# Nine adaLN steps between the output pieces of the spatial gating, attention bias rows on GpSimd's queue a head ahead, row transpositions a step later

## The chip, the cores and the metric

The kernel runs on one core of a Trainium2 chip. A core has five engines with a queue of instructions each, worked through in order: TensorE (PE; its weight loads are listed apart as PEld), VectorE (DVE), ScalarE (ACT), GpSimd (POOL) and SyncE (SP, which here only starts DMA transfers). They meet at semaphores. The metric is device time in microseconds of one execution; less is better.

## The reference: what is computed

A backbone of two layers over 512 latent tokens of width 1024, with 256 context tokens ahead of them. Layer 0 mixes by neighbourhood attention beside chunked spatial gating, layer 1 by retention; each is followed by a gated MLP with a depthwise convolution. What bears on the change:

```
mod_lat = (silu_c @ ada_w[i] + ada_b[i])         # adaLN: 6 x 1024 numbers per stream
mod_ctx = (silu_cc @ ada_w[i] + ada_b[i])        # the same for the context tokens
sh1, sc1, g1, sh2, sc2, g2 = split(mod, 6)
h = modulate(rmsnorm(x, norm_g[i, 0]), sh1, sc1)
y = hybrid_na_sgu(...) or retention_mixer(...)
x = x + g1 * rmsnorm(y, norm_g[i, 1])

# layer 0, the two branches that share one output projection
a_lat = neighbourhood_attention(q, k, v, k_ctx, v_ctx, rpb)   # bias rpb by head, row and column distance
s_lat = spatial_gating(gelu(u), gelu(g), w_s, b_s)            # u * (W_s v + b) in chunks of 128
y = concatenate([a_lat, s_lat]) @ w_out
```

The adaLN vectors depend on the conditioning alone, not on the tokens, so their work may stand anywhere ahead of its use.

## The kernel before

Tokens are held in six tiles of 128 (tiles 4 and 5 are the context). Products are made in three passes on float32r operands: each operand is split into a high part (a copy on ScalarE, line 68) and a low part (a subtraction on VectorE, line 69), and `mm3` (lines 93 to 96) multiplies high by high, high by low and low by high. Weights come in units of 128 x 1024 through three buffers of the tag `raw`, which adaLN's weight loads share.

**adaLN as background steps.** `ada_half(l, half, streams, ...)` makes 512 of the 6 x 1024 numbers of layer l. It is a generator: a call of `self.bg()` runs it to its next `yield`. One step loads a unit of weights (`ar`, issued on SP) and multiplies and adds it on VectorE into an accumulator for each stream (`acc`, line 214: with two streams four operations of 128 x 512). The accumulator is set to zero on GpSimd (line 205) and its first row is loaded with the bias (`in_adab_row`, on SP in layer 0's early halves). After four units the accumulator is split (`ah`, `al`). For the gates (halves 4, 5, 10, 11) a matmul with ones (`ag`, lines 235 and 236) sums it over the partitions and VectorE multiplies it into `G`. For the others a matmul with `sel` (`ac`, line 252) makes two rows, ScalarE copies them (`arow`, line 254), and four small transpositions (`at`, line 259) turn them into columns. When a generator ends, the same call goes on to the first step of the next. Layer 0's jobs are the halves 4, 5 (gates) and 6 to 9; in names such as `acc061`, `ar062` or `al051` the digits are layer, half, and stream or unit.

**Spatial gating (`sgu`).** After the projections and the mixing, twelve output pieces (`out_pieces`, names `wsg`: six token tiles, two halves of the width) of twelve matmuls of 128 x 512 each are run one after the other; ScalarE copies each result (`ysg`, line 492). Ahead of them the loops over the projections call `self.bg()` six times.

**Attention.** Pairs of heads are projected (`project_pair`: `pq`, `px`, `pk`, `pv`, `py`), taken out of PSUM by ScalarE and VectorE (`take_qk`: `q`, `ka`, `kb`, `vt`; GpSimd copies `kb` to its second half, line 773), and then 40 tiles (8 heads of 5 blocks) run through `score` (`s`, then the softmax in `sc` and `sst` on VectorE and ScalarE) and, two tiles later, `weigh` (transpositions `pt`, then `o` and `oc`). Projections of the next pair are filled in between. `self.bg()` is called three times in the first projection and then at every second tile. For each head `bias_tiles` loads a tile `slab` of bias rows (SP, one buffer), scales it on GpSimd (line 798) and adds the masks to make `tm` (lines 803 to 805, two buffers).

**What sets the order.** The source gives priorities, and a scheduler of the tile framework sets each engine's order by dependences, buffers and its own estimates; so a moved step can change which instruction of another kind stands ahead of it. On each engine the order is then fixed.

Retention calls `self.bg()` four times per head for the halves 4 to 9 of layer 1 with one stream; the halves 10 and 11 of both layers and 0 to 3 of layer 1 run in the ConvFFN stages.

Of the kernel before, what the change touches and what calls it, by code (L numbers as in the profile page):

```python
# [8 lines left out]
F32 = mybir.dt.float32  # L9
# [7 lines left out]
P = 128  # L17
# [13 lines left out]
RB = 32  # L31
# [9 lines left out]
class Trunk:  # L41
# [157 lines left out]
    def ada_half(self, l, half, streams, gate=None, away=False, fine=False, side=False):  # L199
        S, V, T, G = self.S, self.V, self.T, self.G  # L200
        m, h = divmod(half, 2)
        acc = []
        for s in range(streams):
            t = (self.lp if s else self.bp).tile([P, 512], F32, name=f"acc{l}{half}{s}", tag=f"acc{s}", bufs=1)
            G.memset(t, 0.0)  # L205
            (G.dma_start if side else self.load)(t[0:1], self.a["adab_row"][l * 12 + half : l * 12 + half + 1])
            acc.append(t)
        for kp in range(4):
            raw = self.bp.tile([P, 1024], F32, name=f"ar{l}{half}{kp}", tag="raw", bufs=3)
            self.load(raw, self.ada_unit_src(l, half, kp))  # L210
            for kk in range(2):
                k = kp * 2 + kk
                for s in range(streams):
                    V.scalar_tensor_tensor(  # L214
                        out=acc[s],
                        in0=raw[:, kk * 512 : kk * 512 + 512],
                        scalar=self.cs[:, 8 * s + k : 8 * s + k + 1],
                        in1=acc[s],
                        op0=ALU.mult,
                        op1=ALU.add,  # L220
                    )
                if fine and kk == 0:
                    yield
            yield
        sp = []
        for s in range(streams):
            hi = self.t2k(f"ah{l}{half}{s}", F32R)
            lo = self.t2k(f"al{l}{half}{s}", F32R)
            self.split(hi, lo, acc[s])
            sp.append((hi, lo))  # L230
            if fine:
                yield
            if m in (2, 5):
                ps = self.ps(f"ag{l}{half}{s}", "C")
                T.matmul(ps, self.ones, hi, start=True, stop=False)
                T.matmul(ps, self.ones, lo, start=False, stop=True)
                ngr = self.t2k(f"ngr{l}{half}{s}")
                row = l * 4 + (1 if m == 2 else 3)
                src = self.a["norm_g"][row : row + 1, h * 512 : h * 512 + 512].broadcast_to([P, 512])
                (G.dma_start if side else self.load)(ngr, src)  # L240
                dst = gate[s][:, h * 512 : h * 512 + 512]
                if away:
                    V.tensor_tensor(out=ngr, in0=ps, in1=ngr, op=ALU.mult)
                    G.dma_start(dst, ngr)
                else:
                    V.tensor_tensor(out=dst, in0=ps, in1=ngr, op=ALU.mult)
        if m in (2, 5):
            return
        ps = self.ps(f"ac{l}{half}", "C")
        n = 2 * streams  # L250
        for i in range(n):
            T.matmul(ps[:2], self.sel[:, i // 2, :], sp[i // 2][i % 2], start=(i == 0), stop=(i == n - 1))
        row = self.t2k(f"arow{l}{half}")
        S.copy(row[:2], ps[:2])
        if fine:
            yield
        pt = self.ps(f"at{l}{half}", "C", (P, 4, 2))
        for i in range(4):
            T.transpose(pt[:, i, :], row[:2, i * P : (i + 1) * P], self.ident[:2, :2])
        ab = self.ab[l, 0 if m < 2 else 1]  # L260
        gi = (l * 4 + (0 if m < 2 else 2)) * 8 + h * 4
        for s in range(streams):
            if m in (0, 3):
                V.tensor_copy(ab[:, s, 1, h * 4 : h * 4 + 4], pt[:, :, s])
            else:
                V.scalar_tensor_tensor(
                    out=ab[:, s, 0, h * 4 : h * 4 + 4],
                    in0=pt[:, :, s],
                    scalar=1.0,
                    in1=self.ng[:, gi : gi + 4],  # L270
                    op0=ALU.add,
                    op1=ALU.mult,
                )
# [279 lines left out]
    def sgu(self, y, xn):  # L553
        S, V, T, G, a = self.S, self.V, self.T, self.G, self.a
        toks = (4, 5, 0, 1, 2, 3)
        with ExitStack() as ctx:
# [105 lines left out]
            mix(1)  # L662
            turn(1)
            pieces = self.out_pieces([(st[0][:, f, :], st[1][:, f, :]) for f in range(4)], wo, y, toks, True, None, "sg")
            for f in pieces:
                f()

    def attention(self, y, final):
        a = self.a
        with ExitStack() as ctx:  # L670
            ap = self.ap = self.phase(ctx, "attp", 0)
            self.mask = ap.tile([P, 3, 256], F32, name="mask", tag="mask")
            self.load(self.mask, a["mask"])
            self.pt_all = ap.tile([P, 4, 4, P], F32, name="ptall", tag="ptall")
            pairs = [{} for _ in range(4)]
            heads = [{} for _ in range(8)]
# [10 lines left out]
            for i in range(n + lag):  # L687
                if i < n:
                    h, b = tiles[i]
# [91 lines left out]
    def take_v(self, j, pr):  # L781
        vn = pr["vn"] = self.ap.tile([P, 6, P], F32, name=f"vn{j}", tag="vn", bufs=1)
        for i, n in ((0, 4), (4, 2)):
# [4 lines left out]
                )  # L788
            self.S.copy(vn[:, i : i + n, :], pv[:, : n * P].rearrange("p (b c) -> p b c", b=n))

    def bias_tiles(self, h, hd):

        G, ap = self.G, self.ap
        tm = hd["tm"] = ap.tile([P, 3, 256], F32, name=f"tm{h}", tag="tm", bufs=2)
        slab = ap.tile([P, 256], F32, name=f"slab{h}", tag="slab", bufs=1)
        z = self.a["rpb"]
        self.load(slab, bass.AP(z.tensor, RB + h * 15 * RB - 8, [[RB, 8], [1, 16], [1, 256]]))
        G.tensor_scalar(out=slab, in0=slab, scalar1=8.0, scalar2=0.0, op0=ALU.mult, op1=ALU.add)
        sr = slab.rearrange("p (r i) -> p i r", r=8)[:, ::-1, ::-1]
        t3 = tm.rearrange("p v (i r) -> p v i r", r=8)  # L800
        m3 = self.mask.rearrange("p v (i r) -> p v i r", r=8)
        for v in range(2):
            G.tensor_tensor(out=t3[:, v], in0=sr, in1=m3[:, v], op=ALU.add)
        G.tensor_tensor(out=t3[:, 2, 0:16], in0=sr[:, 16:32], in1=m3[:, 2, 0:16], op=ALU.add)
        G.tensor_tensor(out=t3[:, 2, 16:32], in0=sr[:, 0:16], in1=m3[:, 2, 16:32], op=ALU.add)

    def score(self, h, b, pr, hd):

# [924 lines left out]
```

## Time and profile before

| what | us |
|---|---|
| median of 3 runs | 1904.04 (1901.92 to 1905.67) |
| the profiled execution | 1893.99 |
| its span on the core | 1892.2 |
| first and last matmul start of the output pieces `wsg` | 118.4, 153.9 |
| first and last matmul start of the scores `s` | 192.8, 365.9 |
| first and last addition of retention's output `yr` (before its last group) | 1119.5, 1395.4 |

The mean granted clock of TensorE in that execution was 0.983 of full speed. In the rows of the profile a name such as `acc<-ar,cs,acc` is output and inputs, `128x512` partitions by elements, and what stands in brackets at a row's end is how long the engine had been idle before it and what ended the wait. A row of the timeline begins with the start and the duration in us. Waits are put down to the semaphore event that came last, so a wait that names an engine which had long been done was for something else, often a DMA.

### The profile page before, as it was taken

The page shows a single profiled execution, that of the slowest core. Times are in us where ns is not written, and L with a number is a line of the kernel's source. Part 1 is how long each engine was busy: PE and PEld are TensorE (multiplying, and loading weights), DVE is VectorE, ACT ScalarE, POOL GpSimd, SP SyncE. Part 2 cuts the span into 40 slices and gives each one's busy share as a digit, 9 for nine tenths or more (in the row PEclk, how much of TensorE's full clock was granted, in tenths as well). Part 3 has the DMA queues.
Part 4 walks back from the last instruction along what each step waited for, and adds up shares of the span by engine and source line. Part 5 has one row for each costly group of instructions (what it writes and reads, how often), then busy time and mean ns, then how long its engine had stood idle before and what let it go on. Part 6 is the DMA issues. An engine that isn't in the chain of part 4 may idle for free. (4 is left out here: it accounts for less than half of the span.)

```text
span 1892.2 us, 28751 instructions
## 1 busy us (share of the span) xinstructions
PE 1800.1 (95%) x10928; PEld 1591.7 (84%) x10928; DVE 1402.8 (74%) x2352; ACT 1029.2 (54%) x1857; POOL 325.8 (17%) x446
## 2 busy tenths in 40 slices
PE   7998989979999999999989999999999989999998
PEld 4886867669889899998879889988989779889996
DVE  4844788679877778777877666675665689989877
ACT  6533545666555555555565434434444377666763
POOL 1102122130122222222121010011011100222221
PEclk9999999999999999999989999999999989999999
DMA  7333332132577877776744313322421225878772
GB/s 290 115 100 106 93 101 79 57 136 76 175 176 156 184 158 167 145 169 135 232 146 131 119 52 112 112 95 62 134 66 48 100 81 148 212 188 195 178 162 99
DMA packets 83823, 250.32 MB, mean 132 GB/s; under 512 B 10578, under 2 KB 12114, under 8 KB 83684
## 3 DMA queue, kind: packets, MB, share of 16 engines
q1 hardware_dynamic: 58436, 200.72, 32.8%
q0 software_dynamic: 25248, 47.75, 15.2%
q8 instruction: 86, 1.41, 0.3%
q14 instruction: 53, 0.43, 0.1%
HBM read 191.81 MB, written 39.85 MB: 122 GB/s over the span
## 5 line engine op out<-in xcount | busy, mean ns | idle before, releaser
L214 DVE SCALAR_TENSOR_TENSOR acc<-ar,cs,acc 128x512 f32<-128x512 f32 x256 | 189.5, 758 | 35.5 <-DMA ar<-in_adaw 19.7
L1463 POOL DMA_DIRECT2D yf<-yp x64 | 55.9, 873 | 260.2 <-ACT yp L1459 229.2
L1314 ACT ACTIVATE cv<-pre,cw 128x770 f32<-128x770 f32 (+1 forms) x88 | 80.9, 923 | 27.2 <-DVE pre L1307 25.9
L1315 DVE SCALAR_TENSOR_TENSOR cv<-pre,cw,cv 128x769 f32<-128x769 f32 (+1 forms) x88 | 77.2, 880 | 7.2 <-ACT cv L1314 7.2
L1459 ACT COPY yp<-wf 128x512 f32<-128x512 f32 x118 | 67.9, 577 | 18.1 <-PE wf L96 18.0
L1318 DVE SCALAR_TENSOR_TENSOR cv<-pre,cw,cv 128x769 f32<-128x769 f32 (+1 forms) x88 | 77.2, 881 | 0.7
L1302 ACT ACTIVATE pre<-px 128x256 f32<-128x256 f32 (+2 forms) x160 | 54.3, 367 | 41.8 <-PE px L93 33.6
L1098 POOL TENSOR_SCALAR rrr<-rmv 128x2 f32<-128x2 f32 x16 | 3.1, 193 | 363.2 <-DVE rmv L1095 363.2
L1463 POOL DMA_DIRECT2D yd<-ypg x48 | 42.1, 903 | 132.1 <-ACT ypg L1459 130.6
L1463 POOL DMA_DIRECT2D yd<-yp x48 | 42.6, 902 | 126.7 <-ACT yp L1459 126.6
L68 ACT ACTIVATE g<-cv 128x770 fp32r<-128x770 f32 (+1 forms) x44 | 32.5, 738 | 32.6 <-DVE cv L1322 32.4
L93 PE MATMUL px<-hs,wd 128*128 128x384 f32 x240 | 45.4, 337 | 0.0
L93 PEld LDWEIGHTS px<-hs,wd 128*128 128x128 f32 x240 | 42.3, 188 | 1.9 <-DVE pre L1307 0.4
L1307 DVE TENSOR_TENSOR pre<-pre,pz 128x256 f32<-128x256 f32 (+1 forms) x60 | 20.8, 371 | 29.2 <-PE pz L96 29.1
L69 DVE TENSOR_TENSOR g<-cv,g 128x770 fp32r<-128x770 f32 (+1 forms) x44 | 36.1, 821 | 7.4 <-ACT g L68 7.3
L1302 ACT ACTIVATE pre<-py 128x384 f32<-128x384 f32 (+1 forms) x40 | 17.5, 437 | 43.9 <-DVE cv L1318 25.6
L1322 DVE TENSOR_TENSOR cv<-cv 128x770 f32<-128x770 f32 (+1 forms) x44 | 36.2, 822 | 4.3 <-ACT cv L1321 3.1
L1321 ACT ACTIVATE cv<-cv 128x770 f32<-128x770 f32 (+1 forms) x44 | 32.7, 742 | 11.7 <-DVE cv L1318 11.6
L1078 DVE SCALAR_TENSOR_TENSOR of<-rx,e,of 128x256 f32<-128x256 f32 x64 | 28.9, 477 | 8.4 <-PE rx L96 7.9
L869 ACT ACTIVATE sc<-sc,sst 128x512 f32<-128x512 f32 x32 | 23.0, 719 | 22.1 <-DVE sc L860 21.6
L1459 ACT COPY ypg<-wf 128x512 f32<-128x512 f32 x54 | 30.7, 578 | 6.5 <-PE wf L96 6.4
L205 POOL MEMSET acc<- 128x512 f32 x32 | 19.1, 600 | 84.5 <-DVE al L69 62.2
(2985 smaller groups left out, 7181.1 us busy)
## 6 DMA issues: line engine op xcount, KB each, us to landing
ar<-in_adaw SPq DMA_DIRECT2D x96, 512.0 KB
yf<-yp POOLq DMA_DIRECT2D x64, 256.0 KB, 4.2
yd<-yp POOLq DMA_DIRECT2D x54, 256.0 KB, 5.2
yd<-ypg POOLq DMA_DIRECT2D x54, 256.0 KB, 5.0
fin<-xd SPq DMA_DIRECT2D x10, 512.0 KB
xd<-xd SPq DMA_DIRECT2D x8, 512.0 KB
xn<-in_x SPq DMA_DIRECT2D x6, 512.0 KB
xb<-in_x SPq DMA_DIRECT2D x6, 512.0 KB
```

Of the source, the lines that this page charges most:

```text
L68: self.S.activation(hi, src, AF.Copy)
L69: self.V.tensor_tensor(out=lo, in0=src, in1=hi.bitcast(F32), op=ALU.subtract)
L93: mm = lambda *p, **k: self.nc.tensor.matmul(*p, skip_group_check=True, **k)
L214: V.scalar_tensor_tensor(out=acc[s], in0=raw[:, kk * 512 : kk * 512 + 512], scalar=self.cs[:, 8 * s + k : 8 * s + k + 1], in1=acc[s], op0= ...
L1302: S.activation(pre[:, i, c : c + w], ps[:, b : b + w], AF.Copy, scale=scale)
L1314: S.activation(d, s, AF.Identity, scale=w1, bias=b)
L1315: V.scalar_tensor_tensor(out=d[:, 1:W], in0=s[:, 0 : W - 1], scalar=w0, in1=d[:, 1:W], op0=ALU.mult, op1=ALU.add)
L1318: V.scalar_tensor_tensor(out=d[:, 0 : W - 1], in0=s[:, 1:W], scalar=w2, in1=d[:, 0 : W - 1], op0=ALU.mult, op1=ALU.add)
L1321: S.activation(cv[:, 0], cv[:, 0], AF.Silu)
L1322: V.tensor_tensor(out=cv[:, 0], in0=cv[:, 0], in1=cv[:, 1], op=ALU.mult)
L1459: S.copy(v, ps)
L1463: G.dma_start((yd[t] if first else y[t])[:, o], v, accum_op=ALU.add)
```

## The change

Three edits. `ada_half` yields between the copy of the row and its transpositions in every job, not only in those called `fine`; a half that isn't a gate so takes five steps instead of four. In `sgu` the loop over the twelve output pieces calls `self.bg()` after each of the first nine. In attention the load of a bias slab moves from SP to GpSimd's queue (`load_slab`), and is issued for the next head at the end of `bias_tiles`, the first one ahead of the loop.

```diff
--- before.py
+++ after.py
@@ -252,8 +252,7 @@
             T.matmul(ps[:2], self.sel[:, i // 2, :], sp[i // 2][i % 2], start=(i == 0), stop=(i == n - 1))
         row = self.t2k(f"arow{l}{half}")
         S.copy(row[:2], ps[:2])
-        if fine:
-            yield
+        yield
         pt = self.ps(f"at{l}{half}", "C", (P, 4, 2))
         for i in range(4):
             T.transpose(pt[:, i, :], row[:2, i * P : (i + 1) * P], self.ident[:2, :2])
@@ -662,8 +661,10 @@
             mix(1)
             turn(1)
             pieces = self.out_pieces([(st[0][:, f, :], st[1][:, f, :]) for f in range(4)], wo, y, toks, True, None, "sg")
-            for f in pieces:
+            for i, f in enumerate(pieces):
                 f()
+                if i < 9:
+                    self.bg()
 
     def attention(self, y, final):
         a = self.a
@@ -671,6 +672,7 @@
             ap = self.ap = self.phase(ctx, "attp", 0)
             self.mask = ap.tile([P, 3, 256], F32, name="mask", tag="mask")
             self.load(self.mask, a["mask"])
+            self.load_slab(0)
             self.pt_all = ap.tile([P, 4, 4, P], F32, name="ptall", tag="ptall")
             pairs = [{} for _ in range(4)]
             heads = [{} for _ in range(8)]
@@ -788,13 +790,16 @@
                 )
             self.S.copy(vn[:, i : i + n, :], pv[:, : n * P].rearrange("p (b c) -> p b c", b=n))
 
+    def load_slab(self, h):
+        self.slab = self.ap.tile([P, 256], F32, name=f"slab{h}", tag="slab", bufs=1)
+        z = self.a["rpb"]
+        self.G.dma_start(self.slab, bass.AP(z.tensor, RB + h * 15 * RB - 8, [[RB, 8], [1, 16], [1, 256]]))
+
     def bias_tiles(self, h, hd):
 
         G, ap = self.G, self.ap
         tm = hd["tm"] = ap.tile([P, 3, 256], F32, name=f"tm{h}", tag="tm", bufs=2)
-        slab = ap.tile([P, 256], F32, name=f"slab{h}", tag="slab", bufs=1)
-        z = self.a["rpb"]
-        self.load(slab, bass.AP(z.tensor, RB + h * 15 * RB - 8, [[RB, 8], [1, 16], [1, 256]]))
+        slab = self.slab
         G.tensor_scalar(out=slab, in0=slab, scalar1=8.0, scalar2=0.0, op0=ALU.mult, op1=ALU.add)
         sr = slab.rearrange("p (r i) -> p i r", r=8)[:, ::-1, ::-1]
         t3 = tm.rearrange("p v (i r) -> p v i r", r=8)
@@ -803,6 +808,8 @@
             G.tensor_tensor(out=t3[:, v], in0=sr, in1=m3[:, v], op=ALU.add)
         G.tensor_tensor(out=t3[:, 2, 0:16], in0=sr[:, 16:32], in1=m3[:, 2, 0:16], op=ALU.add)
         G.tensor_tensor(out=t3[:, 2, 16:32], in0=sr[:, 0:16], in1=m3[:, 2, 16:32], op=ALU.add)
+        if h < 7:
+            self.load_slab(h + 1)
 
     def score(self, h, b, pr, hd):
 
```

By the count of steps, layer 0's jobs ended before in the sixteenth of the calls in attention's loop, and now in the eleventh, with 15 calls instead of 6 ahead of attention. In retention the last step moves from the first call of head 6 to the first call of head 7. Line numbers of the changed kernel are up to seven higher in what follows (`score` L813 is L820, `weigh` L883 is L890), but the transpositions of the row, L259, are L258.

*First place: TensorE, the fourth output piece `wsg51` (token tile 5, second half).* Before:

```order
L94 MATMUL wsg51_1385<-wos2h_1287,sT0_703 128x512
L95 MATMUL wsg51_1385<-wos2l_1288,sT0_703 128x512
L96 MATMUL wsg51_1385<-wos2h_1287,sT1_704 128x512
L94 MATMUL wsg51_1385<-wos3h_1293,sT0_703 128x512
L95 MATMUL wsg51_1385<-wos3l_1294,sT0_703 128x512
L96 MATMUL wsg51_1385<-wos3h_1293,sT1_704 128x512
L94 MATMUL wsg00_1400<-wos0h_1275,sT0_703 128x512
L95 MATMUL wsg00_1400<-wos0l_1276,sT0_703 128x512
```

In the changed kernel:

```order
L94 MATMUL wsg51_1429<-wos2h_1287,sT0_703 128x512
L95 MATMUL wsg51_1429<-wos2l_1288,sT0_703 128x512
L235 MATMUL ag050_1401<-ah050_1397,ones_88 128x512
L96 MATMUL wsg51_1429<-wos2h_1287,sT1_704 128x512
L235 MATMUL ag051_1411<-ah051_1407,ones_88 128x512
L236 MATMUL ag050_1401<-al050_1398,ones_88 128x512
L94 MATMUL wsg51_1429<-wos3h_1293,sT0_703 128x512
L95 MATMUL wsg51_1429<-wos3l_1294,sT0_703 128x512
L236 MATMUL ag051_1411<-al051_1408,ones_88 128x512
L96 MATMUL wsg51_1429<-wos3h_1293,sT1_704 128x512
L94 MATMUL wsg00_1450<-wos0h_1275,sT0_703 128x512
```

The four gate matmuls of half 5 now stand in the end of this piece, ahead of eight more pieces; those of half 6 (`ac06`) come in the piece `wsg21` and its transpositions in `wsg30`.

*Second place: TensorE at the end of the first pair's projection, `pv0` and `py0`.* Before:

```order
L96 MATMUL pv0_1652<-h0a_116,wv0l_1538 128x512
L235 MATMUL ag050_1681<-ah050_1677,ones_88 128x512
L236 MATMUL ag050_1681<-al050_1678,ones_88 128x512
L235 MATMUL ag051_1691<-ah051_1687,ones_88 128x512
L94 MATMUL py0_1709<-h0a_116,wv0h_1537 128x256
L95 MATMUL py0_1709<-h1a_117,wv0h_1537 128x256
```

and, nine rows further on:

```order
L95 MATMUL py0_1709<-h1a_117,wv0h_1537 128x256
L96 MATMUL py0_1709<-h0a_116,wv0l_1538 128x256
L94 MATMUL py0_1709<-h0a_116,wv0h_1537 128x256
L236 MATMUL ag051_1691<-al051_1688,ones_88 128x512
L95 MATMUL py0_1709<-h1a_117,wv0h_1537 128x256
L96 MATMUL py0_1709<-h0a_116,wv0l_1538 128x256
L94 MATMUL py0_1709<-h0a_116,wv0h_1537 128x256
```

In the changed kernel:

```order
L96 MATMUL pv0_1756<-h0a_116,wv0l_1642 128x512
L252 MATMUL ac07_1789<-ah070_1781,sel_90 2x512
L252 MATMUL ac07_1789<-al070_1782,sel_90 2x512
L252 MATMUL ac07_1789<-ah071_1785,sel_90 2x512
L252 MATMUL ac07_1789<-al071_1786,sel_90 2x512
L94 MATMUL py0_1796<-h0a_116,wv0h_1641 128x256
L95 MATMUL py0_1796<-h1a_117,wv0h_1641 128x256
```

Half 5's gate matmuls are gone from here (the last of them stood inside `py0`); the row matmuls of half 7 stand ahead of `py0`. SyncE's queue for the same time, before, from the first weight unit of half 6:

```order
L54 DMA ar060_1703<-in_adaw 128x1024
L54 DMA slab0_1793<-in_rpb 128x1x256
L54 DMA wq1r_1772<-in_hyb_qkv 128x1024
L54 DMA slab1_2028<-in_rpb 128x1x256
L54 DMA wk1r_1778<-in_hyb_qkv 128x1024
L54 DMA ngr050_1684<-in_norm_g 128x512
L54 DMA acc060_1697<-in_adab_row 1x512
L54 DMA slab2_2272<-in_rpb 128x1x256
L54 DMA wv1r_1784<-in_hyb_qkv 128x1024
L54 DMA ar061_1874<-in_adaw 128x1024
L54 DMA ngr051_1694<-in_norm_g 128x512
L54 DMA acc061_1700<-in_adab_row 1x512
```

In the changed kernel, from the third unit of half 7:

```order
L54 DMA ar072_1670<-in_adaw 128x1024
L54 DMA ar073_1726<-in_adaw 128x1024
L54 DMA wq1r_1859<-in_hyb_qkv 128x1024
L54 DMA wk1r_1865<-in_hyb_qkv 128x1024
L54 DMA wv1r_1871<-in_hyb_qkv 128x1024
L54 DMA acc080_1968<-in_adab_row 1x512
L54 DMA ar080_1974<-in_adaw 128x1024
L54 DMA acc081_1971<-in_adab_row 1x512
L54 DMA ar081_2076<-in_adaw 128x1024
L54 DMA ar082_2187<-in_adaw 128x1024
L54 DMA ar083_2273<-in_adaw 128x1024
```

The bias slabs have left this queue, and the weights of pair 1 follow the adaLN loads directly.

*Third place: VectorE at the softmax of head 1's fourth block (`sc13`).* Before, from behind its first instruction to its last:

```order
L771 TENSOR_TENSOR kb11_2148<-pk1_1892,ka11_2147 64x448
L264 COPY ab01_97<-at06_2188 128x4 x2
L214 SCALAR_TENSOR_TENSOR acc070_2195<-ar070_2201,cs_75,acc070_2195 128x512
L771 TENSOR_TENSOR kb11_2148<-px1_1849,ka11_2147 64x256
L771 TENSOR_TENSOR kb11_2148<-pk1_1892,ka11_2147 64x64
L214 SCALAR_TENSOR_TENSOR acc071_2198<-ar070_2201,cs_75,acc071_2198 128x512
L214 SCALAR_TENSOR_TENSOR acc070_2195<-ar070_2201,cs_75,acc070_2195 128x512
L214 SCALAR_TENSOR_TENSOR acc071_2198<-ar070_2201,cs_75,acc071_2198 128x512
L870 RECIPROCAL sst13_2209<-sst13_2209 128x1
L823 TENSOR_REDUCE sst14_2227<-s14_2225 128x2
L871 TENSOR_SCALAR sc13_2208<-sc13_2208,sst13_2209 128x512
```

In the changed kernel:

```order
L69 TENSOR_TENSOR at10_1878<-oc0_2212,at00_1877 64x256
L830 TENSOR_REDUCE sst14_2299<-s14_2297 128x2
L763 TENSOR_TENSOR q11_2246<-pq1_1899,q11_2246 64x512
L766 TENSOR_TENSOR q11_2246<-px1_1936,q11_2246 64x256
L773 TENSOR_TENSOR kb11_2248<-pk1_1992,ka11_2247 64x448
L773 TENSOR_TENSOR kb11_2248<-px1_1936,ka11_2247 64x256
L877 RECIPROCAL sst13_2281<-sst13_2281 128x1
L831 TENSOR_SCALAR sst14_2299<-sst14_2299 128x2
L69 TENSOR_TENSOR al081_2340<-acc081_1971,ah081_2339 128x512
L878 TENSOR_SCALAR sc13_2280<-sc13_2280,sst13_2281 128x512
L773 TENSOR_TENSOR kb11_2248<-pk1_1992,ka11_2247 64x64
```

Before, four accumulations of half 7 stood between the two parts of this softmax; now none stands there, and half 9's follow behind head 2's first block. On GpSimd's queue the load of `slab4` and its scaling now stand between the two memsets of half 9's accumulators, and the scaling of `slab2` ahead of those of half 8.

## The prediction

> **What bounds the kernel now.** I read the page first (busy shares), then the waits of TensorE (PE) in the stretch that the change touches, then busy time in slices there, then the timeline of single engines around each wait.
>
> ```profile
> span 1892.2 us, 28751 instructions
> PE 1800.1 (95%) x10928; PEld 1591.7 (84%) x10928; DVE 1402.8 (74%) x2352; ACT 1029.2 (54%) x1857; POOL 325.8 (17%) x446
> ```
> PE is busy 95% of the span: the kernel is a queue of matmuls, and an edit is worth the PE time that it frees. The change neither adds nor removes a matmul, so only PE's waits count. PE's waits between 100 and 420 us (engine, line, waited for: us in total, times, longest):
>
> ```profile
> PE ag L236 <- DVE al L69: 8.9, 1, 8.9
> PE ht L407 <- DVE ysg L336: 6.5, 3, 4.2
> PE py L94 <- ACT vt L778: 4.4, 2, 3.8
> PE pt L883 <- DVE sst L824: 2.0, 1, 2.0
> ```
> `ht` lies behind attention, in code that the change leaves alone. The other three lie where adaLN steps and bias rows are moved. Slices of 10 us (PE busy, PEld, DVE, ACT, POOL, then the granted clock, DMA share, GB/s):
>
> ```profile
> 140.00:150.00 10.00, 10.00 (x45) 8.07 (x44) 0.00 (x0) 2.00 (x4) 0.00 (x0) 1.00 0.00 0
> 180.00:190.00 10.00, 1.10 (x10) 0.89 (x8) 4.63 (x10) 3.24 (x10) 2.00 (x3) 0.70 0.47 145
> 240.00:250.00 10.00, 7.72 (x41) 4.92 (x40) 9.90 (x28) 3.61 (x10) 2.15 (x1) 1.00 0.36 107
> 270.00:280.00 10.00, 6.21 (x36) 5.45 (x35) 5.31 (x13) 5.77 (x13) 2.26 (x2) 0.83 0.32 93
> ```
> At 140 us, among the output pieces, PE is full and VectorE (DVE) and the DMA engines do nothing: room for adaLN. In attention DVE runs at up to 9.90 of 10 and PE waits.
>
> **Wait 1, 181 to 190 us.**
>
> ```profile
> 190.05 0.80 PE L236 MATMUL ag<-al,ones 128*128 128x512 f32 x1 [8.95 <-DVE al L69]
> 191.29 0.41 PE L95 MATMUL py<-h1a,wv0h 128*128 128x256 f32 x1
> 191.50 0.41 PE L96 MATMUL py<-h0a,wv0l 128*128 128x256 f32 x1
> ...
> 200.55 0.28 PE L95 MATMUL px<-h1a,wq1h 128*128 128x256 f32 x1
> 200.66 0.28 PE L96 MATMUL px<-h0a,wq1l 128*128 128x256 f32 x1
> ```
> PE stands 8.95 us inside `py0` for half 5's last gate matmul. Afterwards matmuls start every 0.21 us instead of 0.11; by the clock (0.50 up to 194) that lasts some 4 us, half of it lost. Price of wait 1: 8.95 + 2.0 = **11.0 us**. Its chain on SyncE's queue (SP), POOL and DVE:
>
> ```profile
> 179.05 0.54 POOL L805 TENSOR_TENSOR tm<-slab,mask 128x128 f32<-128x128 f32 x1
> 179.61 0.64 SPq L54 DMA_DIRECT2D slab<-in_rpb  x1
> 180.87 0.36 SPq L54 DMA_DIRECT2D ar<-in_adaw  x1
> 187.93 0.75 DVE L214 SCALAR_TENSOR_TENSOR acc<-ar,cs,acc 128x512 f32<-128x512 f32 x1 [3.80 <-DMA ar<-in_adaw]
> 189.31 0.68 DVE L69 TENSOR_TENSOR al<-acc,ah 128x512 fp32r<-128x512 f32 x1
> ```
> A bias-row load (`slab2`) sits on SP until GpSimd (POOL) has finished the bias tiles of head 1; the adaLN load behind it goes out at 180.87 and lands 7.1 us later; DVE, in order, waits for it ahead of the split `al051` that PE wants. The change takes out both links: half 5 is finished among the output pieces, and bias rows leave SP. Four matmuls of half 7 (`ac07`) take this place in PE's order, but behind them DVE has eight accumulations whose loads wait for no bias row.
>
> **Wait 2, 243 us.**
>
> ```profile
> 238.12 0.75 DVE L214 SCALAR_TENSOR_TENSOR acc<-ar,cs,acc 128x512 f32<-128x512 f32 x1 [2.74 <-DMA acc<-in_adab_row]
> 242.17 0.48 DVE L871 TENSOR_SCALAR sc<-sc,sst 128x512 f32<-128x512 f32 x1
> 242.79 0.63 PE L883 MATMUL pt<-ident,sc 128*128 128x128 f32 x4 [1.99 <-DVE sst L824]
> ```
> PE waits 1.99 us for the softmax of head 1's fourth block (`sc13`); DVE had lost 2.74 us to half 7's bias row and about 2.8 to four accumulations just ahead of it. In the new order none stands between `sc13`'s first and last instruction (third place above). Price **2.0 us**; the clock stayed at 1.00.
>
> **Wait 3, 271 to 275 us.**
>
> ```profile
> 264.82 0.63 SPq L54 DMA_DIRECT2D slab<-in_rpb  x1
> 265.54 0.41 SPq L54 DMA_DIRECT2D wk3r<-in_hyb_qkv  x1
> 271.04 1.06 ACT L68 ACTIVATE wk3h<-wk3r 128x1024 fp32r<-128x1024 f32 x1 [2.85 <-DMA wk3r<-in_hyb_qkv]
> 274.88 0.39 PE L94 MATMUL py<-h0a,wv2h 128*128 128x256 f32 x1 [3.79 <-ACT vt L778]
> ```
> The same knot: weight `wk3` queued behind `slab5`, ScalarE (ACT) waits for it with the copies of pair 2 behind it, PE waits for those. 3.79 us, and the 0.83 of that slice's clock is 1.7 us more, 1.5 of them after the wait: **5.3 us**. With `slab` gone from SP, `wk3r` follows `wq3r` directly. The same wait one pair later, where no load was late, is the row below, so 0.6 stays and 4.7 goes.
>
> ```profile
> 325.31 0.39 PE L94 MATMUL py<-h0a,wv3h 128*128 128x256 f32 x1 [0.57 <-ACT vt L778]
> ```
> Sum of what goes: 11.0 + 2.0 + 4.7 = 17.7 us.
>
> **What the change adds, part by part.**
>
> *Nine steps between pieces.* They bring eight units of adaLN weights (512 KB each), 32 accumulations, the splits of halves 5 and 6, eight matmuls on a [128x512] row and four small transposes. These only change place; counted with attention, PE's work is the same. What they can add is a wait where PE now reaches an adaLN matmul before DVE.
>
> ```profile
> 161.88 5.53 DVE L214 SCALAR_TENSOR_TENSOR acc<-ar,cs,acc 128x512 f32<-128x512 f32 x8 [2.18 <-DMA ar<-in_adaw]
> ...
> 126.52 0.41 DVE L69 TENSOR_TENSOR sT<-st3C,sT 128x256 fp32r<-128x256 f32 x1
> 156.09 1.23 DVE L69 TENSOR_TENSOR wq0l<-wq0r,wq0h 128x1024 fp32r<-128x1024 f32 x1 [29.16 <-ACT wq0h L68]
> ...
> 150.82 0.59 ACT L492 COPY ysg<-wsg 128x512 f32<-128x512 f32 x1 [2.21 <-PE wsg L96]
> 153.61 0.59 ACT L492 COPY ysg<-wsg 128x512 f32<-128x512 f32 x1 [2.21 <-PE wsg L96]
> ```
> One step is four accumulations of 5.53/8 = 0.69 us, 2.8 us; one piece is 153.61 - 150.82 = 2.79 us. DVE is free from 126.9 to 156.1, 29 us. The two match, so each handover is close:
> - Gate matmuls in `wsg51`: from 126.9, eight accumulations end at 132.5, splits (0.64 on ACT, 0.68 each on DVE) at 134.5. PE would get there at 133 to 134. I take 1.0 us. Below: 0. Above: if both loads take the 7.1 us of the row at 180.87 instead of the 3.6 of the rows below, 4.5.
>
> ```profile
> 115.62 0.33 SPq L54 DMA_DIRECT2D wos1r<-in_hyb_out  x1
> 119.20 1.06 ACT L68 ACTIVATE wos1h<-wos1r 128x1024 fp32r<-128x1024 f32 x1 [2.13 <-DMA wos1r<-in_hyb_out]
> ```
> - Row matmuls `ac06` in `wsg21`: the new accumulator's memset and bias row cost some 2.7 us (the wait of 2.74 above), 16 accumulations 11.1, splits 2: ready at 150.3. PE, with 1.9 us of gate matmuls and wait ahead of it, starts `wsg21` at 150. I take 0.5; 0 to 4.
> - Attention's first weight `wq0l` on DVE, now behind six accumulations of half 7: ready at 160.2 by the same sum, and PE, delayed by twelve moved matmuls and these waits, wants it at 161. I take 0.5; 0 to 4.
>
> *Bias rows on POOL's queue, a head ahead.* SP is rid of eight issues that blocked it. On POOL the issue is hidden under its own idle time (17% busy), but POOL is in order, so what stands behind `slab` waits for its landing: the memsets of `acc08` now stand behind the scaling of `slab2`, then comes their bias row on SP, and `ar080` behind that. In my sum `acc08` starts at 186.5, 4.6 us after DVE ran dry; its 16 accumulations are woven into the first two score tiles, and PE, at `s03`, waits for `sc01` to give its bank back: about 2.5 us. Bounds 0 to 5.4, the latter with the cold clock of wait 3.
>
> The rows show that POOL and DVE slow each other: the same tile operation on POOL takes 870 to 1393 ns.
>
> ```profile
> L803 POOL TENSOR_TENSOR tm<-slab,mask x16: 870/1039/1393, 167.0 to 336.2; 128x256 f32<-128x256 f32 x16
> ```
> The Trainium skill, "SBUF — State Buffer", section "SBUF: two separate sides", says that DVE and GpSimd share one pair of ports under an exclusive lock, and that a DMA issued from GpSimd can starve while DVE holds it. By that rule `slab2`'s issue meets the accumulations of half 7 and lands later; if by two of them (2 x 0.69), `acc08` and `s03` slip by 1.4 us and the sum below is 11.8 instead of 13.2. The row above agrees that the two block each other; no row here shows a slab issue on POOL.
>
> ```profile
> 185.56 0.41 POOL L798 TENSOR_SCALAR slab<-slab 128x256 f32<-128x256 f32 x1 [5.98 <-DMA slab<-in_rpb]
> ```
> POOL waited 6.0 us for this slab. Twice that fits in a head, which lasts (336.2 - 167.0)/7 = 24 us by the tile row's first and last start, so the bias tiles themselves stay early and I add nothing for them.
>
> *Transposes a step later.*
>
> ```profile
> PEld at L259 <- ACT arow L254: 1.3, 4, 0.4
> ```
> The weight loads of the transposes stood 1.3 us in all for the row copy, mostly under a running matmul. I count nothing; bounds -1 to +1. In retention the same edit pushes up to four steps back, into stages like this one, where PE has nothing to gain and DVE has 24 us free of 50; zero, -1 to +2.
>
> ```profile
> 1400.00:1450.00 50.00, 50.00 (x372) 47.23 (x371) 26.20 (x48) 21.69 (x30) 4.51 (x7) 1.00 0.21 65
> ```
> **Sum.** 17.7 - (1.0 + 0.5 + 0.5 + 2.5) = 13.2, so 13 us. The profiled execution (1893.99 us) would become 1881. It is 10 us below the median of the runs shown (1904.04), and the same 13 us off the median give **1891**. ConvFFN stages keep their order.
>
> **Rivals.**
> 1. *The waits move instead of going* (0.20). Wait 1 is taken, but the bias row of `acc09` (its second half stands behind `slab4`) and the late `acc08` make PE stand at `s03` and once more, each past 3.8 us with a cold stretch (2 x 5.3), which more than gives back waits 2 and 3: 17.7 - 2.0 - 10.6 = 5, 1899. For it: DVE's 9.90. Against: some 30 accumulations leave attention. By the Trainium skill, "TensorE: Matmul & The Clock Gate", section "What's actually happening", idling through a window of about 3.4 us halves the clock; waits 2 (1.99, clock 1.00) and 3 (3.79, 0.83) agree, and a new wait of 2 us costs only itself.
> 2. *The stall at `py0` doesn't go* (0.07): `ac07` waits there as `ag05` did, because its loads come late through three shared buffers. Then only waits 2 and 3 are gained, 6.7 - 4.5 = 2: 1902.
> 3. *Slower* (0.06): the DVE chain from 126.9 to `wq0l`. Where PE waits over 3.8 us at each of the three handovers, each costs up to 4.2 + 1.6 cold, 17 in all; with the `s03` wait and waits 2 and 3 unchanged, 11.0 - 17.4 - 2.5 = 9 lost: 1913. It decides once loads land in 7 us instead of 3.6 and DVE gets less than one step per piece. Against: 0.00 DMA share among the pieces.
> 4. *More* (0.07): no new wait at all, the 0.6 us left of wait 3 goes too, and the transposes bring 1 us: 17.7 + 1.6 = 19.3, 1884.7.
>
> **How the numbers follow.** Forecast 0.60: 1887 to 1896, 1891 likeliest. With rival 1 and 4, and most of 2, the range is 1884 to 1902; outside lie rival 3, the top of 2 and some of 4, under 0.2. About 0.2%, 3.8 us, is what a measurement of this kernel can tell from none: faster means below 1900.2. That is forecast and rival 4, 0.67, and three quarters of rival 1, 0.15: 0.82. Same: 0.12 (rival 2 and the rest of 1). Slower: 0.06.
>
> **What would show it.** PE busy above 9.5 of 10 through 180 to 190 with the clock at 1.00, no `slab` on SP, DVE full between 127 and 160, `ac07` without a wait, PE's wait for `vt` under 1 us. Waits of PE for `al` in `wsg51` or `wsg21` above 2 us, for `wq0l`, or at `s03` above 3 us, would make the sum too large; a cold clock at any of them would make it wrong.

## The result and the profile after

| | before | after | ratio |
|---|---|---|---|
| median, runs on one chip | 1903.27 (5 runs, 1899.35 to 1905.67) | 1886.78 (5 runs, 1882.18 to 1895.16) | 0.9927, 95% 0.9902 to 0.9953 |
| the same once more (run 6 below) | 1902.92 (11 runs) | 1884.46 (6 runs, 1880.91 to 1891.07) | 0.9904, 95% 0.9881 to 0.9928 |
| profiled execution | 1893.99 | 1886.89 | |

The changed kernel is 14 to 18 us faster, by the two ratios. Its page, first lines (span, then the busy time of each engine, its share, and the instructions):

```profile
span 1884.7 us, 28785 instructions
...
PE 1801.3 (96%) x10928; PEld 1594.7 (85%) x10928; DVE 1404.0 (74%) x2352; ACT 1028.8 (55%) x1857; POOL 325.9 (17%) x454
```
The busy times are those of before; what shrank is waiting. PE's waits between 100 and 420 us, the two longest (engine, line, waited for: us in total, times, longest):

```profile
PE ht L406 <- DVE ysg L335: 6.0, 3, 3.9
PE pq L94 <- ACT ka L774: 4.7, 1, 4.7
```
The waits for `al` (8.9), `vt` (4.4) and `sst` (2.0) are gone, and a new one of 4.7 us stands at `pq`, the first product of pair 1. The same slices of 10 us as before (busy us of PE, PEld, DVE, ACT and POOL, then PE's granted clock, DMA share, GB/s):

```profile
140.00:150.00 10.00, 10.00 (x45) 7.95 (x44) 9.91 (x16) 2.78 (x5) 0.00 (x0) 1.00 0.45 130
180.00:190.00 10.00, 6.82 (x42) 5.38 (x41) 5.02 (x9) 4.51 (x11) 3.45 (x6) 1.00 0.36 118
190.00:200.00 10.00, 8.07 (x32) 6.64 (x33) 9.91 (x20) 5.61 (x11) 3.93 (x1) 0.83 0.46 129
200.00:210.00 10.00, 10.00 (x63) 8.73 (x63) 7.77 (x22) 2.94 (x6) 0.00 (x0) 1.00 0.60 186
...
240.00:250.00 10.00, 9.93 (x60) 6.91 (x58) 9.94 (x22) 3.43 (x8) 0.00 (x0) 1.00 0.35 105
270.00:280.00 10.00, 9.89 (x58) 6.72 (x57) 7.74 (x23) 6.80 (x14) 2.04 (x2) 1.00 0.14 52
```
DVE, idle at 140 before, is full there now, and PE stays full beside it. At 240 and 270 PE went from 7.72 and 6.21 to 9.9. What is left is the hole from 187 to 192. Its chain, from the timelines of POOL, SP, DVE, ACT and PE:

```profile
180.91 0.63 POOL L796 DMA_DIRECT2D slab<-in_rpb  x1 [0.30 <-POOL tm L810]
184.24 0.40 POOL L803 TENSOR_SCALAR slab<-slab 128x256 f32<-128x256 f32 x1 [2.69 <-DMA slab<-in_rpb]
184.69 0.99 POOL L205 MEMSET acc<- 128x512 f32 x2
...
185.24 0.24 SPq L54 DMA_DIRECT2D acc<-in_adab_row  x1
185.59 0.33 SPq L54 DMA_DIRECT2D ar<-in_adaw  x1
...
189.34 1.42 DVE L214 SCALAR_TENSOR_TENSOR acc<-ar,cs,acc 128x512 f32<-128x512 f32 x2 [4.02 <-DMA ar<-in_adaw]
190.79 0.43 DVE L766 TENSOR_TENSOR q<-px,q 64x256 fp32r<-64x256 f32 x1
...
191.25 0.38 ACT L772 ACTIVATE ka<-px 64x256 fp32r<-64x256 f32 x1 [4.89 <-DVE q L766]
191.65 0.22 ACT L774 ACTIVATE ka<-pk 64x64 fp32r<-64x64 f32 x1
...
191.93 0.80 PE L94 MATMUL pq<-h0a,wq1h 128*128 128x512 f32 x1 [4.68 <-ACT ka L774]
```
Read it downwards. POOL, in order, waits for `slab2` before it zeroes half 8's accumulators. SP, in order, sends their bias row only then, and `ar080` behind it. DVE, in order, stands 4.02 us for `ar080`, with the split `q10<-px0` behind. ACT waits for that split with the last reader of `pk0` behind it, and PE needs this bank for `pq1`. Four queues, each in order, make a load of adaLN, whose matmuls `ac08` PE runs only at 235.66, hold up attention.

To compare kernels free of what happens later, I take the start of the first ConvFFN matmul, `pf`, whose group's row gives the first and last start (before, then after):

```profile
L94 PE MATMUL pf<-hb,wp00h x16: 276/338/522, 411.0 to 1522.0; 128*128 128x384 f32 x8, 128*128 128x256 f32 x8
```
```profile
L94 PE MATMUL pf<-hb,wp00h x16: 274/334/542, 396.4 to 1512.8; 128*128 128x384 f32 x8, 128*128 128x256 f32 x8
```
Up to there the change saves 411.0 - 396.4 = 14.6 us. From there to the end of the span it seems to lose seven (1892.2 - 411.0 = 1481.2, against 1488.3); run 6 settles that.

### The profile page after: what moved, and what is told of

It is laid out like the page before. It is cut to its first block, busy times and chain, and to the rows that moved or that the text cites. A ratio compares the mean times of both kernels' runs of the same rounds, so it can differ in the third digit from the quotient of the medians.

```text
span 1884.7 us, 28785 instructions
## 1 busy us (share of the span) xinstructions
PE 1801.3 (96%) x10928; PEld 1594.7 (85%) x10928; DVE 1404.0 (74%) x2352; ACT 1028.8 (55%) x1857; POOL 325.9 (17%) x454
## 5 line engine op out<-in xcount | busy, mean ns | idle before, releaser
L1466 ACT COPY yp<-wf 128x512 f32<-128x512 f32 x118 | 67.8, 577 | 17.7 <-PE wf L96 17.6
L205 POOL MEMSET acc<- 128x512 f32 x32 | 19.3, 606 | 150.3 <-DVE al L69 131.6
L69 DVE TENSOR_TENSOR rv<-rn,rv 128x512 fp32r<-128x512 f32 x24 | 16.5, 687 | 29.5 <-ACT rv L68 29.5
L68 ACT ACTIVATE rv<-rn 128x512 fp32r<-128x512 f32 x24 | 14.3, 595 | 41.9 <-PE rn L96 41.9
```

What stands on the lines that cost most here:

```text
L68: self.S.activation(hi, src, AF.Copy)
L69: self.V.tensor_tensor(out=lo, in0=src, in1=hi.bitcast(F32), op=ALU.subtract)
L1466: S.copy(v, ps)
```

## The experiments

All runs, in one table (steps: calls among the pieces; later: transpositions a step later; rows: the queue of the bias rows; zero: the engine that zeroes half 8's accumulators). Runs 1 to 4, 5 to 8 and 9 to 12 were each taken together on one chip, with runs of the kernel before beside them.

| run | steps | later | rows | zero | median us | ratio to before, 95% | `pf` at |
|---|---|---|---|---|---|---|---|
| before | 0 | no | SP | POOL | 1902 to 1903 | 1 | 411.0 |
| 9 | 0 | yes | SP | POOL | 1903.15 | 1.0005, 0.9985 to 1.0025 | 411.0 |
| 12 | 9 | no | SP | POOL | 1895.98 | 0.9975, 0.9955 to 0.9994 | 403.5 |
| 1 | 0 | yes | POOL | POOL | 1908.49 | 1.0024, 1.0005 to 1.0043 | 416.9 |
| 3 | 9 | no | POOL | POOL | 1896.13 | 0.9969, 0.9948 to 0.9991 | 405.7 |
| 2 | 9 | yes | SP | POOL | 1886.01 | 0.9912, 0.9885 to 0.9940 | 396.4 |
| change, 6 | 9 | yes | POOL | POOL | 1886.78, 1884.46 | 0.9927, 0.9904 | 396.4, 399.4 |
| 4 | 7 | yes | POOL | POOL | 1890.75 | 0.9931, 0.9906 to 0.9956 | 399.8 |
| 7 | 7 | no | POOL | POOL | 1891.40 | 0.9934, 0.9912 to 0.9957 | 400.2 |
| 8 | 9 | yes | SP | DVE | 1885.69 | 0.9908, 0.9888 to 0.9928 | 397.9 |
| **5** | 9 | yes | POOL | DVE | **1879.97** | 0.9876, 0.9853 to 0.9899 | 391.2 |
| 11 | as 5, `kb` copies on ACT | | | | 1882.67 | 0.9906, 0.9880 to 0.9932 | 394.3 |
| 10 | 0 | yes | POOL | DVE (halves 6 to 8) | 1899.37 | 0.9991, 0.9972 to 1.0010 | 408.4 |

Median less the start of `pf` (one profile each) is 1485 to 1493 in every row, while `pf` itself moves by 26 us, so most of what tells these kernels apart happens ahead of `pf`.

**Run 1: without the steps.**

```diff
-            for i, f in enumerate(pieces):
+            for f in pieces:
                 f()
-                if i < 9:
-                    self.bg()
```


> The change without the nine adaLN steps; bias rows on GpSimd's queue and the later transpositions stay. The prediction's working says that wait 1 hung on two links, a bias row ahead of the adaLN load on SyncE's queue and half 5's gate matmuls standing inside py0. With one link gone the load goes out some 5 us earlier, so that wait 1 shrinks from 8.95 us to 3 to 5 us and its cold stretch goes; wait 3 (3.79 us at py2) goes to under 1 us; wait 2 (2 us) stays. Gain on the kernel before 8 to 12 us, about 1893. Rival (the queue is not what matters, only the room among the pieces): wait 1 stays above 7 us, the gain is 4 to 5 us, 1898.

Slower than the kernel before; both theories fell. Timelines of POOL, SP, DVE and PE:

```profile
182.46 0.40 POOL L801 TENSOR_SCALAR slab<-slab 128x256 f32<-128x256 f32 x1 [2.87 <-DMA slab<-in_rpb]
182.92 0.53 POOL L205 MEMSET acc<- 128x512 f32 x1
...
183.47 0.24 SPq L54 DMA_DIRECT2D acc<-in_adab_row  x1
...
184.82 0.75 DVE L214 SCALAR_TENSOR_TENSOR acc<-ar,cs,acc 128x512 f32<-128x512 f32 x1 [8.08 <-DMA acc<-in_adab_row]
...
194.98 0.79 PE L236 MATMUL ag<-al,ones 128*128 128x512 f32 x1 [13.72 <-DVE al L69]
```
This is the chain of `pq1` again with half 6 in the place of half 8: zeroing behind `slab2`, the row behind the zeroing, DVE's queue behind the row, and `al051` in that queue. Taking the slab off SP didn't break the link; it moved to POOL's queue, where it holds longer (8.95 us of wait before, 13.72 here). Wait 3 went as the theory said, and wait 2, which was to stay, went too.

**Run 2: bias rows as before** (`load_slab` undone; steps and later transpositions stay).

> The change with the bias rows as before, on SyncE's queue and in their own head; the nine steps and the later transpositions stay. Theory (rows on SyncE hold up weights behind them): the new wait at pq1 shrinks, since acc08's memsets stand ahead of slab2 here, but a weight of pair 2 or 3 is held behind slab3 to slab5, and PE waits some 4 us there, as at py2 before: about 3 us slower than the changed kernel, 1890. Rival (the steps alone reorder the queue enough): wk3 now stands ahead of slab5, no weight is late, and the knot at pq1 is gone as well: 4 to 6 us faster than the changed kernel, 1882.

As fast as the changed kernel, where the theory had it 3 us slower, so the rows' move to POOL is worth nothing that these runs can tell. PE waited 1.6 us at `pq` and 2.9 at `s` instead of 4.7 at `pq`: the same knot, against the rival, which was right on the weights. SP's timeline:

```profile
234.22 0.62 SPq L54 DMA_DIRECT2D slab<-in_rpb  x1
...
246.11 0.35 SPq L54 DMA_DIRECT2D wq3r<-in_hyb_qkv  x1
249.99 0.33 SPq L54 DMA_DIRECT2D wk3r<-in_hyb_qkv  x1
...
260.53 0.64 SPq L54 DMA_DIRECT2D slab<-in_rpb  x1
```
With the adaLN jobs further on, `wk3r` stands ahead of `slab5` (before: behind it, at 265.54), and wait 3 is gone with the slabs still on SP.

**Run 3: transpositions in the same step** (`if fine:` back ahead of the `yield`).

> The change with the row transpositions in the same step as before in attention and retention; steps and bias rows as changed. The prediction counted this part at nothing (-1 to +1): then this run is equal to the changed kernel, 1886 to 1888, with a wait of some 4.7 us at pq1. Rival: one step fewer before attention brings all eight accumulations of acc08's first two loads ahead of the split kb00<-pk0 on VectorE, so that the late load holds the whole split of keys: PE waits 8 to 11 us at pq1 with a cold stretch behind it, 6 to 8 us slower than the changed kernel, 1894.

The time is the rival's, spread over more places than it said. PE's waits between 155 and 215 us, and ACT's timeline:

```profile
PE s L821 <- ACT ka L775: 3.6, 1, 3.6
PE pq L94 <- ACT wq0h L68: 3.2, 1, 3.2
PE pq L94 <- ACT vt L781: 2.4, 1, 2.4
```
```profile
192.77 1.06 ACT L68 ACTIVATE wk1h<-wk1r 128x1024 fp32r<-128x1024 f32 x1 [10.72 <-DMA wk1r<-in_hyb_qkv]
```
One step less per row job brings all later adaLN work forward: a unit of half 7 now stands ahead of `wq0r` on SP, and half 8's bias rows ahead of `wk1r`, which goes out at 189.09 instead of 173.05; PE waits for these weights.

**Run 4: seven steps** (`if i < 7:`).

> The change with seven steps among the pieces instead of nine (one number). On VectorE acc08's accumulations now stand behind the last split for pair 0 (kb10<-px0), and its memsets behind the casts on GpSimd. Theory (the wait of 4.7 us at pq1 is the load of acc08 in VectorE's order): PE's wait at pq1 goes to under 0.5 us, the clock stays at 1.00 through 190 to 200, and the kernel is 4 to 6 us faster than the changed one, 1881 to 1883. Rival (pq1 waits for a bank that the splits give back late in any case): the wait stays above 3 us and the time is within 2 us of the changed kernel's.

The wait at `pq1` is gone as the theory said, the time isn't: between two score tiles DVE stands for `ar082` and then runs its four accumulations, 3.1 us, and PE meets that at the transposition of the values (timelines of DVE and PE):

```profile
207.13 1.42 DVE L214 SCALAR_TENSOR_TENSOR acc<-ar,cs,acc 128x512 f32<-128x512 f32 x2 [2.29 <-DMA ar<-in_adaw]
...
212.28 0.69 PE L788 MATMUL vn<-ident,vt 128*128 128x128 f32 x2 [5.29 <-ACT ptall L891]
```
Moving the late accumulations moves the wait.

**Run 5: half 8 zeroed on VectorE.**

```diff
-            G.memset(t, 0.0)
+            (V if (l, half) == (0, 8) else G).memset(t, 0.0)
```


> The changed kernel, with half 8's two accumulators zeroed on VectorE instead of GpSimd; nothing else. In the changed kernel's trace they are zeroed on GpSimd at 184.69, behind the scaling of slab2 that had waited 2.69 us for its load, and the bias row and ar080 go out on SyncE behind that. Here they are zeroed at about 182, and ar080 stands ahead of the bias row on SyncE. Theory (GpSimd's order behind slab2 sets acc08, acc08 holds the splits of pair 0 on VectorE, these hold pq1's bank): VectorE's wait of 4.0 us for ar goes to under 1 us, PE's wait at pq1 from 4.7 to under 1 us, the clock stays at 1.00, 5 to 6 us faster than the changed kernel, 1881. Rival (the time comes back: PE reaches the scores 6 us sooner and VectorE, in its order, does not): a wait of 3 to 5 us at a score or value tile between 200 and 215 us as with seven steps, 1885 to 1887.

As the theory said. DVE's timeline and two slices:

```profile
182.45 0.48 DVE L205 MEMSET acc<- 128x512 f32 x1 [0.17 <-DVE q L763]
...
186.34 0.74 DVE L214 SCALAR_TENSOR_TENSOR acc<-ar,cs,acc 128x512 f32<-128x512 f32 x1
187.11 0.43 DVE L766 TENSOR_TENSOR q<-px,q 64x256 fp32r<-64x256 f32 x1
```
```profile
180.00:190.00 10.00, 8.74 (x52) 7.15 (x51) 9.56 (x18) 6.95 (x18) 5.18 (x6) 1.00 0.45 120
190.00:200.00 10.00, 10.00 (x62) 8.78 (x61) 9.97 (x21) 3.18 (x5) 3.46 (x1) 1.00 0.66 189
```
The accumulation starts at 186.34 without a wait, the split follows at 187.11 instead of 190.79, PE has no wait left at `pq`, and only 1.3 us at `s` for `kb`. This kernel beats the changed one by 4.5 us of median on the same chip (1877.76 to 1881.16 against 1880.91 to 1891.07); the intervals of the two ratios overlap a little, but `pf` starts at 391.2, 5 us and more ahead of both profiles of the change.

**Run 6: the change again.**

> The changed kernel itself once more, to have it on the same chip as the others. Theory: 0.991 to 0.994 of the kernel before, with the first matmul of ConvFFN's block 0 (pf) at 396 to 397 us of the span, as in the first profile, and the stretch from there to the end anywhere between 1481 and 1495 us, which is what the six profiles so far show of work in one and the same order. Rival (the change slows ConvFFN): that stretch is over 1488 us again.

The rival fell: from `pf` to the end it takes 1880.7 - 399.4 = 1481.3 us here, as before the change; over the ten profiles with the later transpositions, and so with one order from `pf` on (the change, runs 1, 2, 4 to 6 and 8 to 11), it is anywhere from 1481 to 1495; over the four with the order of before (before, runs 3, 7 and 12) from 1481 to 1493. So the seven microseconds need no cause in the change, and the kernel before had a lucky execution (1893.99 against a median of 1903). The theory missed the start of `pf`, by 3 us, and the ratio, 0.9904, by a little: the wait at `pq` was 4.8, nearly the same, with one of 1.3 for `kb` just ahead of it, but the clock behind it stayed low far longer (slices of its profile):

```profile
180.00:190.00 10.00, 7.65 (x46) 6.08 (x44) 6.10 (x9) 4.52 (x11) 5.19 (x7) 0.98 0.25 71
190.00:200.00 10.00, 6.18 (x15) 4.94 (x16) 8.67 (x17) 4.92 (x10) 3.93 (x1) 0.51 0.43 147
```

**Run 7: seven steps, transpositions in the same step** (`if i < 7:`, and `if fine:` as in run 3), so that half 8 stands on DVE as in the changed kernel.

> Seven steps among the pieces and row transpositions in the same step as before; bias rows as changed. On VectorE acc08 then stands where it does in the changed kernel (two accumulations ahead of q10<-px0), against eight ahead of kb00<-pk0 with nine steps and early transpositions. Theory (the later transpositions count only as two steps of the sequence): equal to the changed kernel or up to 3 us faster, since ar080 stands ahead of the bias row here; 1884 to 1887, no wait of PE above 5 us between 155 and 210. Rival (the transposition itself, waiting for its row copy in PE's order, is what costs): as with nine steps and early transpositions, 1894 to 1897, with a wait at the transposition of 1 us and more.

Between the two. Timelines of ACT and PE:

```profile
203.09 1.04 ACT L68 ACTIVATE wq2h<-wq2r 128x1024 fp32r<-128x1024 f32 x1
204.04 0.56 ACT L254 COPY arow<-ac 2x512 f32<-2x512 f32 x1
...
204.65 0.40 PE L259 MATMUL at<-ident,arow 2*128 2x2 f32 x4 [3.51 <-ACT arow L254]
```
So the later transpositions do two things. They count as steps (run 3 against run 7: 5 us of median, though not taken side by side), and they keep PE from standing at `at` while ACT has the row copy behind other work, 3.51 us here and a cold stretch (TensorE at half clock) behind it. PE also waits 3.5 us at `s` for `kb` here, and no run shows how much of the 7 us to the changed kernel each makes.

**Run 8: rows on SyncE, zeroed on VectorE** (run 2 with the line of run 5).

> Bias rows on SyncE in their own head, as before the change, and half 8's accumulators zeroed on VectorE; steps and transpositions as changed. Theory (two links in a row, the zeroing on GpSimd and the queue on SyncE): with the zeroing gone from GpSimd the row slab2 on SyncE still waits for the bias tiles of head 1 (until about 183), ar080 behind it lands at about 187.5, and PE still waits 3 to 4 us at pq1 or for the keys: 1885, within 2 us of the same kernel with zeroing on GpSimd. So the bias rows' move is worth some 5 us, but only together with the zeroing on VectorE. Rival (the zeroing alone is the knot): as good as the changed kernel with zeroing on VectorE, 1881.

As the theory said; PE waits 1.0 us at `pq` and 3.9 at `s`. SP and DVE:

```profile
183.88 0.63 SPq L54 DMA_DIRECT2D slab<-in_rpb  x1
184.61 0.40 SPq L54 DMA_DIRECT2D ar<-in_adaw  x1
...
190.33 0.82 DVE L214 SCALAR_TENSOR_TENSOR acc<-ar,cs,acc 128x512 f32<-128x512 f32 x1 [4.40 <-DMA ar<-in_adaw]
```
Two links in a row: against run 2, which has both, taking out either one alone (the change: SP; run 8: the zeroing) gains nothing; taking out both (run 5) gains 5 us.

**Run 9: the later transpositions alone, on the kernel before.**

> The kernel before, with the later transpositions alone. Theory (they matter only where the steps have pulled a transposition among work that it can hold up): within 3 us of the kernel before, 1900 to 1905, with the wait of 8.9 us at half 5's gate matmul unchanged. Rival (each transposition that waits for its row copy costs PE, in retention too): 4 us faster or more, 1898 or less.

No difference, as expected, but not because nothing happened. Slices of its profile:

```profile
240.00:250.00 10.00, 10.00 (x60) 7.35 (x58) 9.92 (x28) 3.27 (x7) 0.00 (x0) 1.00 0.29 84
270.00:280.00 10.00, 9.88 (x59) 6.94 (x58) 7.13 (x23) 6.73 (x15) 1.37 (x2) 1.00 0.19 53
...
340.00:350.00 10.00, 6.76 (x42) 4.86 (x40) 9.64 (x28) 6.37 (x14) 0.00 (x0) 0.92 0.34 93
```
Waits 2 and 3 are gone here too, but as much is lost later, in waits for the softmax among others: from 325 to 365 us PE loses 8.0 us to idling and the half clock, against 2.0 before (8.53 of 10 in the slice from 340 before, 6.76 here). Runs 1 and 10, which also lack the steps, show the same 8 us there; in the changed kernel it is 0.9.

**Run 10: no steps, halves 6 to 8 zeroed on VectorE.**

> The change without the nine steps (that was 1908), with the accumulators of halves 6, 7 and 8 zeroed on VectorE. Theory (the wait of 13.7 us at half 5's gate matmul came from acc06, zeroed on GpSimd behind slab2 at 182.92, which held VectorE's queue for 8.1 us ahead of al051): the 8.1 us wait of VectorE goes to under 1 us, al051 ends at 187 to 188 instead of 194.9, PE waits 6 to 7 us there; 6 to 9 us faster than without the zeroing, 1900 to 1903, still 13 us and more behind the kernel that has the steps too. Rival (al051 is late because of VectorE's own load in attention): wait at the gate matmul over 11 us, 1906 and more.

Theory right, and the wait shrank further than it said: `al` is split at 186.72, PE's wait at `ag` is 4.8 instead of 13.7. Zeroing on GpSimd behind a slab cost 6 us there by the two ratios, 9 by the medians, which were taken on two chips; the steps stay worth about 20 (0.9991 against 0.9876; here halves 6 and 7 are zeroed on VectorE as well).

**Run 11: `kb` copies on ScalarE,** on top of run 5 (`S.copy` for `G.tensor_copy` at the end of `take_qk`).

> The changed kernel with half 8 zeroed on VectorE (that was 1880), and the copies of the keys' low halves (kb) on ScalarE instead of GpSimd. In the traces such a copy takes GpSimd 0.82 us, but 3.9 to 4.6 us where VectorE's accumulations run beside it, and PE waited 1.3 us for it at the first score tile. Theory (the two engines slow each other): that wait goes, VectorE's accumulations there lose nothing, 1 to 2 us faster, 1878 to 1880. Rival (ScalarE has these copies in front of vt and the first exponential): PE waits there instead, 1881 to 1884.

The rival: PE waits 1.8 us at `pq` and 1.2 at `s`; 2.7 us above run 5, not taken side by side. No gain.

**Run 12: the nine steps alone, on the kernel before.**

> The kernel before with the nine steps alone: bias rows in their own head on SyncE's queue, transpositions in the same step. Theory (steps and later transpositions belong together: with early transpositions eight accumulations of acc08 stand ahead of the split of pair 0's keys): 1892 to 1898, as with the bias rows moved and early transpositions (1896). Rival (the steps are the whole gain): 1885 to 1888.

As the theory said. PE waits 3.2 us for `wq0h` at `pq` and 2.3 at `s`, as in run 3. Steps alone bring 5 to 6 us, later transpositions alone nothing, both together 16 (run 2).

## Why the prediction was right, and where it was not

*The sum.* It forecast 13 us; the two ratios give 14 and 18, the starts of `pf` 14.6 and 11.6. That the profiled execution of before stood 10 us under its median, and the gain was to be taken off the median, held; as far as one profile tells, the 10 us lay behind `pf`, where its 1481.2 is the least of all the profiles.

*The three waits* went, and with wait 3 the 0.6 us that was to stay: no wait for `vt` is listed. The reason for **wait 3** was wrong: "With `slab` gone from SP, `wk3r` follows `wq3r` directly" is true, but the slab's move isn't needed: in runs 2, 9 and 12 the slabs are still on SP, and wait 3 is gone with the steps, with the later transpositions or with both. For **wait 1** it named two links and took both as cut. Run 1 shows that the second, off SP, came back on POOL's queue; what ends wait 1 is that half 5 is finished among the pieces.

*The handovers among the pieces* (1.0 + 0.5 + 0.5) were too dear: no wait for `ag` or `ac` is listed, and `wq0l` cost 0.3. The times were near (the last splits for `ag` and `ac` end at 134.8 and 152.1, `wq0l` at 160.4, against 134.5, 150.3 and 160.2), but PE has matmuls of the pieces to run between those of adaLN.

```profile
PE pq L96 <- DVE wq0l L69: 0.3, 1, 0.3
```
*The late `acc08`* is the term that was mis-sized: "about 2.5 us" at `s03`, bounds 0 to 5.4. Its cause was named rightly (memsets behind the scaling of `slab2`), its place not. At `s03` PE waits for nothing (10.00 of 10 from 200 on). `acc08` started at 189.34, not 186.5, and PE waits 4.68 us at `pq1`, because two accumulations stand ahead of `q10<-px0`, and 1.7 us more go to the half clock until 195.3: 6.4, or 7.8 in run 6. So the prediction's own sign, PE above 9.5 of 10 from 180 to 190, failed (6.82).

*That the sum came so close is in part luck.* With the measured prices in its place it would be 17.7 - (0.3 + 6.4) = 11.0, further from the 14.6 at `pf` than the forecast. What makes up for it was not in the sum. Adding idle time and what the half clock costs, in slices of 1 us, PE loses 19.0 us from 180 to 285 before and 7.0 after, and 2.3 against 1.0 from 285 to 365, where the prediction saw no gain. With 0.3 lost at `wq0l` that is 13.0 of the 14.6; the rest is not placed.

*Transpositions a step later*, "I count nothing", holds alone (run 9) and fails in company: without them the change gives 6 us (run 3). They are a part of the gain that the prediction had booked to the other two edits. A diff's parts were priced one by one, while in a fixed sequence of steps each part sets what the others meet.

*Rival 1*, waits that move, was the right worry: it happened in runs 3, 4, 7 and 9. Of the rule on the shared port, the prediction said that `slab2`'s issue on POOL would meet accumulations and land later by two of them. It met none: no accumulation runs on DVE from 175.7 to 189.3, and the issue at 180.91 was followed by the scaling 3.33 us later. The issue of `slab1` met them, and its scaling followed after 3.65 us, so a cost like that did not show:

```profile
171.46 0.65 POOL L796 DMA_DIRECT2D slab<-in_rpb  x1 [0.30 <-POOL tm L810]
175.11 0.83 POOL L803 TENSOR_SCALAR slab<-slab 128x256 f32<-128x256 f32 x1 [3.00 <-DMA slab<-in_rpb]
...
169.75 5.93 DVE L214 SCALAR_TENSOR_TENSOR acc<-ar,cs,acc 128x512 f32<-128x512 f32 x8
```
What did show is POOL's copy of `kb`, slowed beside DVE's accumulations:

```profile
185.74 0.82 POOL L775 CAST kb<-kb 64x768 fp32r<-64x768 f32 x1
192.54 3.93 POOL L775 CAST kb<-kb 64x768 fp32r<-64x768 f32 x1 [5.98 <-DVE kb L773]
...
192.40 3.39 DVE L214 SCALAR_TENSOR_TENSOR acc<-ar,cs,acc 128x512 f32<-128x512 f32 x5
```
The copy begins beside five accumulations and ends 0.7 us behind them (at 196.47 and 195.79). By the Trainium skill, "SBUF — State Buffer", section "SBUF: two separate sides", whichever of the two engines starts first, VectorE with two inputs in SBUF or GpSimd reading it, holds the shared ports for its whole instruction. These rows agree that one keeps the other out, but for a whole row of accumulations, not for one of 0.69 us: 3.1 us are added to a copy of 0.82.

## What to carry to other kernels

Where several in-order queues are chained, list for each late load every queue that it passes: cutting one link gains nothing while another holds (run 8, and the change against run 2), and cutting the last one gains at once (run 5). Background work woven into a sequence is priced by what stands behind it in each queue, not by its own length; a zeroing of 0.99 us in the wrong queue cost some 5 us. And compare profiles at a milestone behind the changed part, since the rest of this one, in one and the same order, varied by 13 us between executions.

## What was not expected of the hardware

The low clock came in pieces of 3.4 us. A slice's granted clock below 1.00 gives the time spent at half: 2 x (1 - 0.83) x 10 = 3.4 us in the slice from 190 of the changed kernel, whereas in run 6, after nearly the same wait, 0.98 and 0.51 in the slices from 180 and 190 make 10.2, three times as much; run 8 shows 0.66, twice 3.4. The Trainium skill, "TensorE: Matmul & The Clock Gate", section "What's actually happening", has a window of about 3.4 us that runs free of the program; the multiples agree. So nearly the same wait, 4.68 and 4.85 us, cost 1.7 us more in one execution and 2.9 in the other. Slices of 1 us fit a difference of phase: in the changed kernel the clock fell at 191.8, as the wait ended, and came back 3.4 us later; in run 6 it fell at 189.5, 4.3 us ahead of the wait's end at 193.8, and came back after three pieces, at 199.8; the third was the first that PE was busy throughout. But run 6 also had a wait of 1.33 us just ahead, and no run has the two apart. Waits of 1.8 us (run 11) and 1.99 us (before) cost only themselves, while one of 3.19 us in run 3 brought a piece of 3.4 (0.83 in the slice from 160).
